# Weight sums of the last projection made in the first layer and stored, and attention units recorded to end one chunk ahead of their host

## The chip, the cores and the metric

The kernel runs on one core of one Trainium2 chip. The metric is the device time of one execution in microseconds (us). Engines are named as the profile names them: PE (TensorE matmuls), PEld (its weight loads), DVE (VectorE), ACT (ScalarE), POOL (GpSimd), SP (SyncE, which issues every DMA of this kernel).

## What is computed

A decoder trunk of two layers on x, 1024 positions of 1024 features, float32. The reference, cut:

```python
for i in range(DEPTH):                          # DEPTH = 2
    if i < N_A_LAYERS:                          # layer 0: retention, 4 heads, qk 256, v 512
        u = rms_norm(h, ret_norm_pre[i])
        q, k, v, g = jnp.split(u @ ret_w_in[i], ...)
        o = retention_chunkwise(rope(q), rope(k) * 256 ** -0.5, v)      # per head, normed
        y = (merge_heads(o) * silu(g)) @ ret_w_out[i]                   # first output projection
        h = h + rms_norm(y, ret_norm_post[i])
        k_sh, v_sh = jnp.split(rms_norm(h, kv_norm) @ w_kv, [SB_QK_WIDTH], axis=-1)
    else:                                       # layer 1: stick-breaking attention, 8 heads
        q, g = jnp.split(rms_norm(h, sb_norm_pre[j]) @ sb_w_in[j], [SB_QK_WIDTH], axis=-1)
        z = q @ k_sh.T * scale
        A = sigmoid(z) * (product of 1 - sigmoid(z) over the later keys), strictly causal
        y = (merge_heads(A @ v_sh) * silu(g)) @ sb_w_out[j]             # second output projection
        h = h + rms_norm(y, sb_norm_post[j])
```

## The kernel before

Each of the large products is a 2x2 block product done with seven block products instead of eight (numbered 1 to 7), each operand of which is a sum or difference of blocks. Every float32 operand is split into a rounded part ("hi") and the rest ("lo"), and a product is three matmuls (`mm3`: hi by hi, hi by lo, lo by hi). ACT makes the hi part, DVE the lo part.

The class `Out` does an output projection (2048 to 1024). It has 28 units `(n, i)`: block product n in the order 1, 5, 3, 6, 7, 4, 2, and i, one of four quarters of the block's 1024 contracted rows. For a unit, `weights(n, i)` loads one or two blocks of 128 x 1024 into tiles `raw`, adds them on DVE where the product needs a sum, and splits the result into a tile `whl`; `operand(n, i)` does the same for the activations (`raw` to `op`, or to `AT` for n = 2). The sums of the weights are w10+w11 for product 5, w10+w11+w00 for 6, w01 plus that for 3, and w10+w00 for 7: four adds of 128 x 1024 for each i. `Out` is used twice: in the first layer (base 48) and at the end of the second (base 112, operands `oc`). A unit is two chunks (`kk`) of 4 x 3 matmuls of 512 columns.

The class `Group` does the input projections, six groups in each layer: in the first layer v0, g0, k, q, v1, g1 (in this order, with the products 2 and 7 of v0, g0 and v1 ahead of all), in the second K, Q, V0, G0, V1, G1.

Attention in the second layer goes by 16 units: 8 pairs of heads and position halves `(t, pr)`, two heads `hh` each. For a unit, `CPair.rows` makes four row blocks of 128 queries: scores on PE (tile `pz` from `ko`, `ko`), two sigmoids on ACT into tiles `n` (named `sgn`, or `f` for t = 0) and `a` (named `A`, or `f`), two causal selects on POOL, then on DVE a running product over `sgn` (a scan) and the product `A<-A,sgn`. `CPair.mix` then turns blocks of A with PE transposes (`pz<-ident,A`), splits them into `AT` (ACT hi, DVE lo), and multiplies with the values into `po`; at its end `gate` multiplies `po` with the gate into `S` and stores it to `oc`. Units with t = 1 have 1024 keys and are the heavy ones.

Attention has no stage of its own: it is recorded between the chunks of a host by `merge(main, *sides)`. Each side is `(steps, lead, tail)`; after chunk i of the host's len(main), as many of the steps are recorded as their share of the chunks from `lead` to len(main) - `tail`. While unit k is mixed, the rows of unit k + 1 are made (`head(k)`). Units 0 to 3 are hosted by V1's products, units 4 to 7 by G1's, units 8 to 15 by half products of the last projection, four chunks each.

What is recorded is not yet the order on the engines. `Recorder` keeps the list of operations, and `Plan` simulates the engines with costs written by hand and gives every engine its order: PE may take an operation from up to 100 ahead, the other engines take whichever of their ready operations has the earliest deadline. `limits` makes the deadlines backwards from the time of the PE operations. Tiles come from tagged pools of a fixed number of buffers: `raw` shares a pool of 28 with `xh`, `v`, `A`, `AT`, `S`, `ko` and `sgn`. The instruction stream of an engine is fixed by this, and so is SP's order of DMAs.

Of the kernel before, what the change touches and what calls it, by code (L numbers as in the profile page):

```python
# [10 lines left out]
F32 = mybir.dt.float32  # L11
F32R = mybir.dt.float32r
AF = mybir.ActivationFunctionType
ALU = mybir.AluOpType
# [26 lines left out]
DMA_QUEUE = 2000.0  # L41
DMA_TIME = 4000.0
PE_AHEAD = 100


class Tile:
# [95 lines left out]
class Recorder:  # L142
    def __init__(self, nc):
        self.nc, self.ops, self.turning, self.placed = nc, [], False, set()
        for e, name in enumerate(ENGINES):
            setattr(self, name, Engine(self, e, name))

# [7 lines left out]
    def add(self, engine, method, args, kw):  # L155
        o = Op()
        o.i, o.engine, o.method, o.args, o.kw = len(self.ops), engine, method, args, kw
        views = [x for x in list(args) + list(kw.values()) if isinstance(x, View)]
        out, also = args[0], kw.get("accum_out")
        o.deps, o.tiles = set(), []  # L160
        for x in views:
            if x.tile not in o.tiles:
                o.tiles.append(x.tile)
        for x in views:
            t, m, w = x.tile, x.mask(), x is out or x is also
            for j, jm, jw in t.log:
                if jm & m and (w or jw):
                    o.deps.add(j)
        for x in views:
            t, m, w = x.tile, x.mask(), x is out or x is also  # L170
            if w:
                t.log = [(j, jm & ~m, jw) for j, jm, jw in t.log if jm & ~m]
            t.log.append((o.i, m, w))
        o.deps.discard(o.i)
        self.cost(o, out, [x for x in views if x is not out and x is not also])
        for t in o.tiles:
            t.users += 1
        self.ops.append(o)
# [102 lines left out]
class Plan:  # L281
# [23 lines left out]
                        self.reuse[j].append(first)  # L305
    def limits(self, when, end):
        late = [0.0] * len(self.ops)
        for o in reversed(self.ops):
            x = when[o.i] if o.engine == PEE else end
            took = DMA_TIME if o.engine == SPE else o.took  # L310
            for j in self.succ[o.i]:
                x = min(x, late[j] - took - 40)
            for j in self.reuse[o.i]:
                x = min(x, late[j] - took - 40)
            late[o.i] = x
        return late
# [140 lines left out]
def trunk(ctx, tc, xT, wts, gains, trig, ident_in, cols, grow_in, out):  # L457
# [471 lines left out]
    class Out:  # L929

        def __init__(self, base, o_d, turned, y, put):
            self.base, self.o_d, self.turned, self.y, self.put = base, o_d, turned, y, put
            self.units = [(n, i) for n in (1, 5, 3, 6, 7, 4, 2) for i in range(4)]
            self.get = ahead(28, lambda at: (self.weights(*self.units[at]), self.operand(*self.units[at])))
            self.banks, self.kept, self.s, self.x = {}, {}, {}, {}

        def pieces(self, x):
            return x[:, 0, :], x[:, 1, :]

        def weights(self, n, i):  # L940

            def load(j, half):
                raw = S("raw", [1024])
                dma(raw[:], wts[self.base + 8 * j + 4 * half + i])
                return raw

            def plus(a, b):
                V.tensor_tensor(a[:], a[:], b[:], ALU.add)
                return a

            w = S("whl", [2, 1024], F32R)
            if n in (1, 2, 4):
                a = load(*{1: (0, 0), 2: (0, 1), 4: (1, 1)}[n])
            elif n == 7:
                a = plus(load(1, 0), load(0, 0))
            elif n == 6:
                a = self.s[i]
            elif n == 5:
                a = self.s[i] = plus(load(1, 0), load(1, 1))
            else:  # L960
                a = plus(self.s[i], load(0, 0))
                a = plus(load(0, 1), a)
            split(self.pieces(w), a[:])
            return w
# [576 lines left out]
    def run():  # L1541
# [24 lines left out]
        def unit(k):  # L1566

            def sides():
                x = [(U[k].mix() + U[k].give + U[k].gate(), 0, 0)]
                if k < 7:  # L1570
                    x.append((U[k + 1].scores(), 0, 0))
                return x
            return sides
        main = groups[0].chunks(2)
        X.load(1, 0, (1,))
        X.unnormed(1, 0)
# [15 lines left out]
        for at, group in enumerate(groups):  # L1592
# [7 lines left out]
            else:  # L1600
                if at == 2:
                    X.tables()
                go(group.chunks(*order[at]))
        hold, acc = [[None] * 4 for _ in range(2)], [[], []]

        def held(t, j, b):
# [22 lines left out]

        def head(k):  # L1630
            h, hh = seq[k]
            x = [(P[h].mix(hh), 0, 0)]
            if k + 1 < len(seq):
                h, hh = seq[k + 1]
                x.append((P[h].rows(hh), 0, 0))
            return x
        for at, group in enumerate(groups[:4]):
            go(group.chunks(*order[at]), (lambda: [(late[2:], 0, 16)]) if at == 0 else None)
        for at, first in ((4, 0), (5, 4)):
            n = order[at]  # L1640
# [1 line left out]
            for k in range(4):  # L1642
                go(groups[at].chunks(n[k + 1]), lambda k=k: head(first + k))
            go(groups[at].chunks(n[5]))
        turns, done = zip(*[finish(t) for t in range(2)])
        Y = Out(112, oc_d, True, lambda t, j, b: S("f2", [512])[:], lambda t, j, b, y: done[t](j, b, y))
        for k, n in enumerate((1, 5, 3, 6)):
            for half in range(2):
                go(Y.chunks(n)[4 * half:4 * half + 4], lambda k=k, half=half: head(8 + 2 * k + half))
# [69 lines left out]
```

## Time and profile before

| what | value |
|---|---|
| time, median of three runs (lowest, highest) | 1589.07 us (1587.85, 1589.58) |
| the profiled execution: its time, its span | 1590.58 us, 1588.8 us |
| PE busy in the span | 1572.9 us, 7416 matmuls |
| DVE busy | 1306.5 us, 1909 instructions |
| ACT, POOL busy | 831.1 us, 230.2 us |
| DMA, mean | 253 GB/s, 401.62 MB |

The span reaches from the first to the last instruction; the execution's time has 1.8 us more. A matmul in the records lasts longer than the next one has to wait, so two matmuls overlap in the records, and "busy" is the union. What a stall of PE takes is read from the starts of neighbouring matmuls.

### The profile page before, as it was taken

The page shows a single profiled execution, that of the slowest core. Times are in us where ns is not written, and L with a number is a line of the kernel's source. Part 1 is how long each engine was busy: PE and PEld are TensorE (multiplying, and loading weights), DVE is VectorE, ACT ScalarE, POOL GpSimd, SP SyncE. Part 2 cuts the span into 40 slices and gives each one's busy share as a digit, 9 for nine tenths or more (in the row PEclk, how much of TensorE's full clock was granted, in tenths as well). Part 3 has the DMA queues.
Part 4 walks back from the last instruction along what each step waited for, and adds up shares of the span by engine and source line. Part 5 has one row for each costly group of instructions (what it writes and reads, how often), then busy time and mean ns, then how long its engine had stood idle before and what let it go on. Part 6 is the DMA issues. An engine that isn't in the chain of part 4 may idle for free. (4 is left out here: it accounts for less than half of the span.)

```text
span 1588.8 us, 22243 instructions
## 1 busy us (share of the span) xinstructions
PE 1572.9 (99%) x7416; PEld 1303.5 (82%) x7416; DVE 1306.5 (82%) x1909; ACT 831.1 (52%) x1470; POOL 230.2 (14%) x298
## 2 busy tenths in 40 slices
PE   9999999999999999999999999999999999999998
PEld 7888888888887888888888888888888888878886
DVE  6997779797677988999989856757778889899897
ACT  7643432323566665546665554545555654455464
POOL 0000015140022432310000000001211211222000
PEclk9999999999999999999999999999999999999999
DMA  8775737388457887875686968768789778787674
GB/s 286 250 250 184 232 113 232 113 279 290 164 175 241 301 334 273 311 299 171 202 301 231 335 218 318 251 223 280 267 283 338 266 278 285 299 291 270 253 268 156
DMA packets 173490, 401.62 MB, mean 253 GB/s; under 512 B 19520, under 2 KB 20160, under 8 KB 173376
## 3 DMA queue, kind: packets, MB, share of 16 engines
q1 hardware_dynamic: 173376, 400.21, 71.5%
q8 instruction: 58, 0.95, 0.2%
q14 instruction: 56, 0.46, 0.1%
HBM read 295.28 MB, written 104.86 MB: 252 GB/s over the span
## 5 line engine op out<-in xcount | busy, mean ns | idle before, releaser
L228 ACT ACTIVATE whl<-wraw 128x512 fp32r<-128x512 f32 (+1 forms) x264 | 157.3, 626 | 233.8 <-PE po L228 69.9
L228 DVE TENSOR_TENSOR whl<-wraw,whl 128x512 fp32r<-128x512 f32 x264 | 183.7, 720 | 92.1 <-ACT whl L228 91.2
L228 PE MATMUL pma<-whl,xh 128*128 128x512 f32 x480 | 126.3, 394 | 0.7 <-DVE whl L228 0.5
L228 PE MATMUL pmb<-whl,xh 128*128 128x512 f32 x480 | 123.6, 390 | 0.0
L228 PE MATMUL pma<-xh,whl 128*128 128x512 f32 x408 | 104.8, 391 | 0.8 <-DVE f L228 0.8
L228 PEld LDWEIGHTS pmb<-whl,xh 128*128 128x128 f32 x480 | 89.8, 188 | 18.6
L228 PE MATMUL pmb<-xh,whl 128*128 128x512 f32 x408 | 104.7, 390 | 0.0
L228 PEld LDWEIGHTS pma<-whl,xh 128*128 128x128 f32 x480 | 88.2, 188 | 18.9 <-DVE whl L228 0.9
L228 PE MATMUL pz<-ko,ko 128*128 128x384 f32 (+3 forms) x480 | 96.2, 327 | 0.0
L228 POOL TENSOR_SCALAR_AFFINE_SELECT f<-f 128x128 f32<-128x128 f32 x64 | 35.3, 566 | 405.1 <-DMA g<-sg 285.2
L228 ACT ACTIVATE AT<-pz 128x512 fp32r<-128x512 f32 (+1 forms) x96 | 45.0, 490 | 89.6 <-PE pz L228 88.9
L228 PEld LDWEIGHTS pma<-xh,whl 128*128 128x128 f32 x408 | 76.1, 188 | 16.7 <-DVE f L228 1.2
L228 POOL TENSOR_TENSOR f<-f,f 128x512 f32<-128x512 f32 x32 | 53.2, 1672 | 252.4 <-DVE f L228 225.1
L228 PE MATMUL pma<-op,whl 128*128 128x512 f32 x336 | 89.5, 396 | 0.0
L228 PEld LDWEIGHTS pmb<-xh,whl 128*128 128x128 f32 x408 | 76.2, 188 | 15.8 <-DVE f L228 0.2
L228 DVE SCALAR_TENSOR_TENSOR wraw<-wraw,gn,wraw 128x512 f32<-128x512 f32 x96 | 71.0, 746 | 19.7 <-ACT wraw L228 9.5
L228 PE MATMUL pmb<-op,whl 128*128 128x512 f32 x336 | 86.5, 391 | 0.0
L228 PEld LDWEIGHTS pz<-ko,ko 128*128 128x128 f32 x480 | 76.3, 190 | 11.7 <-DVE AT L228 1.7
L228 DVE TENSOR_TENSOR wraw<-wraw,wraw 128x512 f32<-128x512 f32 x96 | 69.9, 747 | 13.2 <-DMA wraw<-in_wts_dram 12.8
L228 PE MATMUL pz<-xh,whl 128*128 128x512 f32 x312 | 79.4, 389 | 0.0
L228 PE MATMUL po<-xh,whl 128*128 128x512 f32 x312 | 79.2, 389 | 0.0
L228 PE MATMUL pma<-whl,op 128*128 128x512 f32 x288 | 78.4, 399 | 0.0
(220 smaller groups left out, 3654.5 us busy)
## 6 DMA issues: line engine op xcount, KB each, us to landing
wraw<-in_wts_dram SPq DMA_DIRECT2D x431, 256.0 KB, 5.1
raw<-in_wts_dram SPq DMA_DIRECT2D x72, 512.0 KB, 7.0
v<-v SPq DMA_DIRECT2D x64, 512.0 KB, 5.3
ko<-kq SPq DMA_DIRECT2D x40, 512.0 KB, 5.7
raw<-o SPq DMA_DIRECT2D x36, 512.0 KB, 7.0
raw<-oc SPq DMA_DIRECT2D x36, 512.0 KB, 6.2
kq<-v SPq DMA_DIRECT2D x32, 512.0 KB, 6.5
s<-f SPq DMA_DIRECT2D x40, 256.0 KB, 3.1
```

Source lines behind the costliest of these rows:

```text
L228: f(*[_real(a) for a in o.args], **{k: _real(v) for k, v in o.kw.items()})
```

## The change

It has two parts. First, `Out.add(i)` makes the four weight sums of the second layer's projection for one i: it loads the four blocks, adds them in place with four DVE instructions, and stores each sum to a DRAM tile `ws`. The four calls are recorded in the first layer beside the rest of g0 (i = 0), k (i = 1, 2) and q (i = 3); their operations are marked `filler`, and `limits` gives a filler a deadline of its own, 15 us (`FILL`, in ns) behind the next PE operation in the recorded order. `weights` then loads the stored sum where there is one. So 16 adds leave the last projection, its weight loads go from 36 to 28 (the 16 sums, and 12 plain blocks), and 16 adds, 16 loads and 16 stores, of 512 KB each, are new in the first layer. Second, `head` gives both of its sides a tail of 1: a unit's mixing and the next unit's rows are recorded over the host's chunks but the last.

```diff
+FILL = 15000.0
...
     def limits(self, when, end):
         late = [0.0] * len(self.ops)
+        turn = end
         for o in reversed(self.ops):
-            x = when[o.i] if o.engine == PEE else end
+            if o.engine == PEE:
+                turn = when[o.i]
+            x = when[o.i] if o.engine == PEE else min(end, turn + FILL) if o.filler else end
...
+        def load(self, j, half, i):
+            raw = S("raw", [1024])
+            dma(raw[:], wts[self.base + 8 * j + 4 * half + i])
+            return raw
+
+        def add(self, i):
+            rec.filler = True
+            a, b, c, d = [self.load(j, half, i) for j, half in ((1, 0), (1, 1), (0, 0), (0, 1))]
+            for n, x, y in ((5, b, a), (7, a, c), (6, c, b), (3, d, c)):
+                V.tensor_tensor(x[:], x[:], y[:], ALU.add)
+                self.sums[n, i] = DRAM(f"ws{self.base}{n}{i}", F32)
+                dma(self.sums[n, i][:], x[:])
+            rec.filler = False
...
         def weights(self, n, i):
...
-            if n in (1, 2, 4):
+            if (n, i) in self.sums:
+                a = S("raw", [1024])
+                dma(a[:], self.sums[n, i][:])
+            elif n in (1, 2, 4):
...
+        Z = Out(112, oc_d, True, lambda t, j, b: S("f2", [512])[:], lambda t, j, b, y: done[t](j, b, y))
...
-                go(group.chunks(*order[at]))
+                go(group.chunks(*order[at]), (lambda at=at: [([Z.adds()[i] for i in {1: (0,), 2: (1, 2), 3: (3,)}[at]], 2, 2)]) if at in {1: (0,), 2: (1, 2), 3: (3,)} else None)
...
         def head(k):
             h, hh = seq[k]
-            x = [(P[h].mix(hh), 0, 0)]
+            x = [(P[h].mix(hh), 0, 1)]
             if k + 1 < len(seq):
                 h, hh = seq[k + 1]
-                x.append((P[h].rows(hh), 0, 0))
+                x.append((P[h].rows(hh), 0, 1))
...
-        Y = Out(112, oc_d, True, lambda t, j, b: S("f2", [512])[:], lambda t, j, b, y: done[t](j, b, y))
+        Y = Z
```

Both parts move instructions through the planner. PE's order is the same as before from the start up to the first of the second layer's attention units (about 1105 us in the profile), and another from there on. DVE's, ACT's and SP's orders differ in the first layer from about 112 us to 312 us, are the same up to about 1100 us, and differ from there. POOL's instructions stand in the same order of kinds throughout. In the rows below a name is the program's (`A2544` is the tile `A` number 2544; what follows the underscore is the build's own number); tiles of the two kernels have different numbers.

The first place is PE where a heavy unit begins to be mixed, the first of those hosted by the last projection (about 1403 us before). Before:

```order
L228 MATMUL pma2460_13448<-whl2528_13822,op2532_13794 128x512
L228 MATMUL pma2461_13454<-whl2528_13822,op2532_13794 128x512 x3
L228 MATMUL pmb2462_13466<-whl2528_13822,op2532_13794 128x512 x3
L228 MATMUL pmb2463_13472<-whl2528_13822,op2532_13794 128x512 x3
L228 MATMUL pz2554_13898<-ident_68,A2544_13873 128x128
L228 MATMUL pz2557_13903<-ident_68,A2544_13873 128x128
L228 MATMUL po2569_13939<-AT2555_13933,vo2553_13732 128x512
```

and after, on the same engine, at the same unit:

```order
L231 MATMUL pma2475_13541<-whl2545_13780,op2548_13788 128x512 x2
L231 MATMUL pmb2476_13549<-whl2545_13780,op2548_13788 128x512 x2
L231 MATMUL pz2564_13983<-ident_68,A2551_13931 128x128
L231 MATMUL pz2567_13986<-ident_68,A2551_13931 128x128
L231 MATMUL pmb2476_13549<-whl2545_13780,op2548_13788 128x512
L231 MATMUL pmb2477_13555<-whl2545_13780,op2548_13788 128x512 x3
L231 MATMUL po2572_14020<-AT2565_14010,vo2563_13666 128x512
```

The transposes of the unit's last row block stood right ahead of the first product `po` that needs them; now four of the host's matmuls stand between.

The second place is DVE ahead of the same point (about 1392 to 1405 us before): the scans and products that make the last two row blocks. Before:

```order
L228 TENSOR_TENSOR AT2534_13786<-pz2533_13781,AT2534_13786 128x128
L228 TENSOR_TENSOR raw2530_13683<-raw2530_13683,raw2436_13041 128x1024
L228 TENSOR_TENSOR A2524_13756<-A2524_13756,sgn2525_13751 128x767
L228 TENSOR_TENSOR op2532_13794<-raw2531_13741,op2532_13794 128x1024
L228 TENSOR_TENSOR whl2528_13822<-raw2530_13683,whl2528_13822 128x1024
L228 SCALAR_TENSOR_TENSOR sgn2536_13813<-sgn2536_13813 128x896
L228 TENSOR_TENSOR S2543_13881<-po2520_13726,sg2522_13704 128x512
L228 TENSOR_TENSOR S2543_13881<-po2521_13734,sg2523_13717 128x512
L228 TENSOR_TENSOR A2535_13817<-A2535_13817,sgn2536_13813 128x895
L228 SCALAR_TENSOR_TENSOR sgn2545_13867<-sgn2545_13867 128x1024
L228 TENSOR_TENSOR raw2455_13192<-raw2455_13192,raw2549_13808 128x1024
L228 TENSOR_TENSOR A2544_13873<-A2544_13873,sgn2545_13867 128x1023
```

and after:

```order
L231 SCALAR_TENSOR_TENSOR sgn2527_13800<-sgn2527_13800 128x640
L231 TENSOR_TENSOR A2526_13806<-A2526_13806,sgn2527_13800 128x639
L231 SCALAR_TENSOR_TENSOR sgn2539_13849<-sgn2539_13849 128x768
L231 TENSOR_TENSOR A2538_13855<-A2538_13855,sgn2539_13849 128x767
L231 TENSOR_TENSOR S2549_13904<-po2532_13804,sg2534_13646 128x512
L231 TENSOR_TENSOR S2549_13904<-po2533_13811,sg2535_13659 128x512
L231 TENSOR_TENSOR whl2559_13892<-raw2560_13840,whl2559_13892 128x1024
L231 SCALAR_TENSOR_TENSOR sgn2543_13874<-sgn2543_13874 128x896
L231 SCALAR_TENSOR_TENSOR sgn2552_13926<-sgn2552_13926 128x1024
L231 TENSOR_TENSOR A2542_13881<-A2542_13881,sgn2543_13874 128x895
L231 TENSOR_TENSOR A2551_13931<-A2551_13931,sgn2552_13926 128x1023
L231 TENSOR_TENSOR op2562_13936<-raw2561_13858,op2562_13936 128x1024
```

The two weight adds (`raw<-raw,raw`) that stood in this stretch are gone, and the scans of the last two row blocks stand directly behind each other.

The third place is DVE in the first layer, beside g0 (about 146 to 152 us before). Before:

```order
L228 TENSOR_TENSOR whl271_1747<-wraw253_1548,whl271_1747 128x512
L228 TENSOR_TENSOR whl271_1747<-wraw256_1591,whl271_1747 128x512
L228 TENSOR_TENSOR wraw277_1736<-wraw277_1736,wraw243_1464 128x512
L228 SCALAR_TENSOR_TENSOR f2264_1775<-f2258_1613,col102_864,f2263_1770 128x512
L228 SCALAR_TENSOR_TENSOR f2266_1782<-f2259_1644,col102_864,f2265_1777 128x512
```

and after:

```order
L231 TENSOR_TENSOR raw297_1691<-raw297_1691,raw296_1590 128x1024
L231 TENSOR_TENSOR raw296_1590<-raw296_1590,raw298_1703 128x1024
L231 TENSOR_TENSOR whl271_1772<-wraw253_1566,whl271_1772 128x512
L231 TENSOR_TENSOR whl271_1772<-wraw256_1614,whl271_1772 128x512
L231 TENSOR_TENSOR raw298_1703<-raw298_1703,raw297_1691 128x1024
L231 TENSOR_TENSOR raw361_1750<-raw361_1750,raw360_1732 128x1024
L231 TENSOR_TENSOR wraw277_1776<-wraw277_1776,wraw243_1480 128x512
L231 SCALAR_TENSOR_TENSOR f2264_1819<-f2258_1660,col102_880,f2263_1800 128x512
```

Four of the 16 new adds are set between the splits of g0's weights. Counted along DVE's order, 13 of the 16 stand ahead of what ran at about 228 us before, the other three where 247 to 275 us were.

More of the change, by code (lines that the diff above doesn't have):

```diff
@@ L144, in __init__ @@
         self.nc, self.ops, self.turning, self.placed = nc, [], False, set()
+        self.filler = False
         for e, name in enumerate(ENGINES):
@@ L157, in add @@
         o.i, o.engine, o.method, o.args, o.kw = len(self.ops), engine, method, args, kw
+        o.filler = self.filler
         views = [x for x in list(args) + list(kw.values()) if isinstance(x, View)]
@@ L935, in __init__, with adds @@
             self.banks, self.kept, self.s, self.x = {}, {}, {}, {}
+            self.sums = {}
         def pieces(self, x):
             return x[:, 0, :], x[:, 1, :]
+        def load(self, j, half, i):
[10 more added lines that the diff above has]
+            rec.filler = False
+        def adds(self):
+            return [lambda i=i: self.add(i) for i in range(4)]
         def weights(self, n, i):
             def load(j, half):
-                raw = S("raw", [1024])
-                dma(raw[:], wts[self.base + 8 * j + 4 * half + i])
-                return raw
+                return self.load(j, half, i)
             def plus(a, b):
@@ L1573, in unit @@
             return sides
+        turns, done = zip(*[finish(t) for t in range(2)])
+        Z = Out(112, oc_d, True, lambda t, j, b: S("f2", [512])[:], lambda t, j, b, y: done[t](j, b, y))
         main = groups[0].chunks(2)
@@ L1644, in run @@
             go(groups[at].chunks(n[5]))
-        turns, done = zip(*[finish(t) for t in range(2)])
-        Y = Out(112, oc_d, True, lambda t, j, b: S("f2", [512])[:], lambda t, j, b, y: done[t](j, b, y))
+        Y = Z
         for k, n in enumerate((1, 5, 3, 6)):
```

## Prediction

> **What bounds the kernel now.** I read the page first, then busy time by stretches, then PE's waits, then PE's and DVE's instructions around each wait.
>
> ```profile
> span 1588.8 us, 22243 instructions
> PE 1572.9 (99%) x7416; PEld 1303.5 (82%) x7416; DVE 1306.5 (82%) x1909; ACT 831.1 (52%) x1470; POOL 230.2 (14%) x298
> ```
>
> PE is the bound: 15.9 us of the span are without a matmul, and neither part of the change adds or removes a matmul. So only PE's stalls can move the time. By stretches (length, then busy time and count of each engine, granted clock, DMA share, GB/s):
>
> ```profile
> 10.00:1095.00 1085.00, 1082.08 (x4945) 894.88 (x4944) 884.26 (x1358) 558.52 (x938) 150.64 (x166) 1.00 0.70 245
> 1190.00:1250.00 60.00, 58.44 (x291) 47.75 (x291) 53.86 (x70) 37.75 (x75) 10.25 (x14) 1.00 0.87 313
> 1408.00:1412.00 4.00, 4.00 (x17) 3.35 (x16) 3.45 (x3) 1.51 (x6) 1.74 (x2) 0.57 0.79 261
> 1582.00:1589.00 7.00, 0.12 (x1) 0.00 (x0) 2.96 (x5) 1.02 (x3) 0.00 (x0) 0.76 0.20 75
> ```
>
> 6.9 us are the end behind the last matmul, which the change leaves alone; 2.9 us lie in the 1085 us before the second layer's attention. What remains is short, and sits in the attention's stretch. PE's waits from 1095 us to the end (total, times, longest), and below them the one kind that the first layer's hosted units (430 to 700 us) show:
>
> ```profile
> PE po L228 <- ACT AT L228: 1.7, 3, 0.6
> PE pz L228 <- DVE A L228: 0.9, 1, 0.9
> PE pma L228 <- DVE f L228: 0.8, 1, 0.8
> PE po L228 <- ACT sgn L228: 2.1, 3, 0.9
> ```
>
> Matmuls overlap in the records, so a wait costs more than its idle time; the loss is read from starts. The pace of 128x512 matmuls that wait for nothing, from the chain at the end, is 11.00/48 = 0.229 us:
>
> ```profile
> 1560.25 11.00 PE pma L228 x48
> ```
>
> PE's instructions in order of time, at the five places that lose most (start, length, what, idle before and its releaser):
>
> ```profile
> 1190.98 2.89 PE L228 MATMUL pma<-xh,whl 128*128 128x512 f32 x12
> 1194.66 1.66 PE L228 MATMUL pma<-xh,whl 128*128 128x512 f32 x6 [0.79 <-DVE f L228]
> ...
> 1223.27 0.86 PE L228 MATMUL pma<-xh,whl 128*128 128x512 f32 x3
> 1224.33 0.30 PE L228 MATMUL pz<-ident,A 128*128 128x128 f32 x1 [0.20 <-DVE AT L228]
> ...
> 1237.35 0.38 PE L228 MATMUL pz<-ident,A 128*128 128x128 f32 x2
> 1238.31 0.73 PE L228 MATMUL po<-AT,vo 128*128 128x512 f32 x2 [0.58 <-ACT AT L228]
> ...
> 1403.27 1.55 PE L228 MATMUL pmb<-whl,op 128*128 128x512 f32 x6
> 1405.67 0.44 PE L228 MATMUL pz<-ident,A 128*128 128x128 f32 x2 [0.85 <-DVE A L228]
> 1406.69 0.74 PE L228 MATMUL po<-AT,vo 128*128 128x512 f32 x2 [0.58 <-ACT AT L228]
> ...
> 1411.08 1.24 PE L228 MATMUL pz<-ident,A 128*128 128x128 f32 x8
> 1412.08 1.86 PE L228 MATMUL po<-AT,vo 128*128 128x512 f32 x7
> ...
> 1437.25 0.38 PE L228 MATMUL pz<-ident,A 128*128 128x128 f32 x2
> 1438.21 0.73 PE L228 MATMUL po<-AT,vo 128*128 128x512 f32 x2 [0.58 <-ACT AT L228]
> ```
>
> Losses, start to start: (a) where G1's matmuls follow V1's, 1194.66 - 1190.98 - 12 x 0.229 = 0.93 us; (b) 1224.33 - 1223.27 - 3 x 0.229 = 0.37 us; (c) transposes straight ahead of the `po` that needs them, three times: 0.96, 1.02 and 0.96 us, of which two transposes may take 2 x 1.00/8 = 0.25 (the row of eight), so 0.71 + 0.77 + 0.71 = 2.19 us; (d) the late row block, 1405.67 - 1403.27 - 6 x 0.229 = 1.03 us; (e) behind it the granted clock is 0.57 over 4 us (the third stretch above), which loses 4 x 0.43 = 1.72 us. Sum: 6.24 us.
>
> What made (d) late stands in DVE's order of time:
>
> ```profile
> 1398.82 1.26 DVE L228 TENSOR_TENSOR S<-po,sg 128x512 f32<-128x512 f32 x2
> 1400.00 1.07 DVE L228 TENSOR_TENSOR A<-A,sgn 128x895 f32<-128x895 f32 x1
> 1400.99 2.37 DVE L228 TENSOR_TENSOR_SCAN sgn<-sgn 128x1024 f32<-128x1024 f32 x1
> 1403.29 1.19 DVE L228 TENSOR_TENSOR raw<-raw,raw 128x1024 f32<-128x1024 f32 x1
> 1404.41 1.21 DVE L228 TENSOR_TENSOR A<-A,sgn 128x1023 f32<-128x1023 f32 x1
> ```
>
> DVE runs without a pause there, and a weight add of 1.12 us (start to start) stands between the last scan and the product that PE's transposes wait for.
>
> **The adds leave the last projection.** In the stretch that hosts attention and the last projection, DVE is busy
>
> ```profile
> 1376.00:1560.00 184.00, 181.99 (x934) 151.38 (x932) 169.23 (x188) 104.90 (x192) 24.52 (x34) 0.99 0.76 277
> L228 DVE TENSOR_TENSOR raw<-raw,raw 128x1024 f32<-128x1024 f32 x18 | 21.9, 1220 | 0.0
> ```
>
> 169.2 of 184 us (92%). Of these 18 adds, those of weights go (16 in the whole projection, 16 x 1.22 = 19.5 us). DVE falls to some 82 to 85%. Eight weight loads of 512 KB go as well. Taking the adds away ends (d): the product could start 1.12 us earlier, more than the 1.03 us lost, and DVE's rows of the new order show five adds fewer between the storing of the unit before (`S`) and this product. With (d) go the two holes in 3 us that stand ahead of the slow clock, so (e) goes too. Together 2.75 us.
>
> [...]
>
> **The tail of one chunk.** A unit's rows end a chunk earlier, and its host's last chunk stands alone behind them. PE's rows of the new order show it twice. Where a heavy unit begins, four host matmuls stand between the last transposes and the first `po` (in the seven heavy hand-offs: four each, five once). They cover 4 x 0.229 = 0.92 us, against holes of 0.71 to 0.77: all of (c) goes, 2.19 us. And where G1 follows V1, PE before ran four groups of three matmuls into one bank while it waited for DVE to empty another; now the banks follow each other in turn, and the last scores stand some 40 host matmuls earlier, so DVE's scans no longer collide with emptying the banks: (a) goes, 0.93 us. For (b), a transpose late by 0.37 us, bounds are 0 and 0.37; I take 0.37, since DVE has less to do there too. What is late next: the last two row blocks, whose scans now stand back to back (below).
>
> **The adds in the first layer.** 16 adds, 16 loads and 16 stores are new where PE waits for nothing. The room:
>
> ```profile
> 125.00:235.00 110.00, 110.00 (x487) 91.13 (x486) 79.69 (x122) 42.61 (x74) 6.68 (x4) 1.00 0.53 176
> 235.00:310.00 75.00, 75.00 (x332) 62.12 (x331) 64.28 (x88) 23.45 (x40) 26.34 (x16) 1.00 0.55 183
> 349.88 1.67 POOL L228 TENSOR_TENSOR f<-f,f 128x512 f32<-128x512 f32 x1 [7.93 <-DVE f L228]
> 350.31 1.78 DVE L228 TENSOR_TENSOR wraw<-wraw,wraw 128x512 f32<-128x512 f32 x1
> ```
>
> DVE is idle 30.3 us in the first stretch, which gets 13 adds (15.9 us), and 10.7 us in the second, which gets three (3.7 us). The 32 transfers are 16.8 MB; at 176/0.53 = 332 GB/s they take 51 us, and DMA is free for 0.47 x 110 + 0.45 x 75 = 85 us. SP issues 32 more DMAs, and a store that waits for its add holds the weight loads behind it, for the length of an add or two. The last two rows show the danger, an add that took 1.78 us beside one of 1.67 on POOL. POOL is busy 6.7 us in the first stretch; if all of it falls on new adds they take 15.9 + 6.7 = 22.6 of the 30.3 us. In the second, one POOL add on each of the three makes 3.7 + 5.0 = 8.7 of 10.7. I cost this part at 0; what hides it is the weights made ahead, and without that cover an add late by its whole length costs 1.2 us each. Bounds: 0 to 3 us lost, a gain excluded, since PE has no hole there to fill.
>
> **The sum.** 6.24 us of losses go. A new order has holes of its own: none seen at the hand-offs, so 0 is one end; the other is the first layer's hosted units, 2.1 us of waits in 270 us, which over the 494 us from 1095 on is 3.8 us. I take 1.0, nearer to 0, because the hand-offs are covered by rows of the order. Net 6.24 - 1.0 = 5.2 us. On the profiled execution (1590.58 us, its span 1588.8 and 1.8 around it) that gives 1585.4; the median of the runs shown is 1.5 us below it, and I predict 1589.07 - 5.2 = 1583.9 us.
>
> **Rivals.** Against the median, 0.2% (3.2 us) is about what a measurement of this kernel can tell from no change.
>
> *Moved, not removed.* The new order has as many holes as the hosted units of the first layer, 3.8 us, or (e) comes back at another hole: gain 6.24 - 3.8 = 2.4 us, 1586.7 us. For it: PE's order is new over 494 us, and a single hole pair like 1403 to 1412 costs 1.03 + 0.77 + 1.72 = 3.5 us. Against: every heavy hand-off has its cover.
>
> *The slow clock stays.* If (e) hangs on something other than the holes ahead of it, 5.2 - 1.7 = 3.5 us are left, 1585.6 us. The row speaks against it, and no other row for it; a chance of 0.08, inside the forecast's.
>
> *Nothing of the adds.* DVE is at 92% either way one may say, and (d) is the latency of scan and product; then only (a) and (c) go, 3.1 us: 1586.0 us. Against it stands the add of 1.12 us in the row itself.
>
> *Slower.* The last two row blocks' scans stand back to back: 2.37 us of the last scan and the product of the block before (1.07) now lie between a scan and its own product. If at the heavy hand-offs the last product comes later than PE's transposes, each costs a hole and a clock drop like (d) with (e), 2.75 us, and from the third on the change loses: 6.24 - 4 x 2.75 = -4.8, so four of seven give 1593.8 us. For it: the order's pairs. Against: the last product there has no add ahead of it, and its transposes stand later on PE than before.
>
> *All goes and nothing comes:* 6.24 us and up to 2 us more of small waits between: 1581 to 1583 us.
>
> **Chances.** Forecast (gain 3.2 to 6.2 us) 0.48; all goes 0.18; moved or nothing of the adds 0.26, of which a little lies above 3.2; slower 0.08. Faster by over 0.2%: 0.67; within: 0.25; slower: 0.08. The likeliest case's own range is 1582.9 to 1585.9; the range that leaves out the slower case and the outer half of "all goes" is 1580.8 to 1589.4.
>
> **What the profile after would show.** PE's waits from 1095 us: no `po` on `AT` at 0.58, no `pz` on `A`, sum below 1.5 us instead of 3.6; granted clock 1.00 up to the last matmul; DVE at 82 to 85% from 1376 to 1560 us; in the first layer raw adds beside PE at 100%. The prediction is wrong if PE waits for `whl` between 125 and 350 us, if the clock drops at another place, or if `pz` waits for `A` at the hand-offs.

## The result and the profile after

The changed kernel takes 1583.89 us (median of six runs, 1582.14 to 1585.25), beside 1589.32 us for the kernel before in runs taken with it (1587.85 to 1591.66). The ratio is 0.9966, with a 95% interval of 0.9955 to 0.9976: 5.4 us less. The forecast was 1583.9 us. The profiled execution took 1583.15 us, with a span of 1581.3 us. One further execution of the kernel before, run beside the experiments, took 3201.51 us and is left out of every figure below.

The top of the page of the kernel after:

```profile
span 1581.3 us, 22235 instructions
PE 1570.2 (99%) x7416; PEld 1302.4 (82%) x7416; DVE 1308.4 (83%) x1909; ACT 830.1 (52%) x1470; POOL 225.9 (14%) x298
```

PE's and DVE's busy times hardly differ from before (1572.9 and 1306.5 us); 11.1 us of the span are now without a matmul, where 15.9 us were. What moved stands in the stretches. Kernel after, busy time by stretches, in the columns of the prediction's:

```profile
1190.00:1250.00 60.00, 60.00 (x302) 49.40 (x302) 50.67 (x69) 36.65 (x72) 7.87 (x12) 1.00 0.86 306
1400.00:1412.00 12.00, 12.00 (x65) 9.82 (x64) 8.63 (x12) 7.01 (x13) 0.54 (x2) 1.00 0.89 330
1376.00:1560.00 184.00, 184.00 (x950) 153.05 (x949) 158.97 (x188) 107.35 (x202) 17.61 (x33) 1.00 0.69 252
125.00:235.00 110.00, 110.00 (x487) 91.10 (x487) 92.93 (x133) 41.66 (x72) 6.54 (x4) 1.00 0.88 307
235.00:310.00 75.00, 75.00 (x333) 62.13 (x331) 69.32 (x91) 23.49 (x40) 28.54 (x16) 1.00 0.63 208
```

In the 60 us around G1's beginning PE has no idle time left (before: 1.6 us), nor in the 184 us of the last projection (before: 2.0 us); the granted clock is 1.00 there, and in the 12 us around the hand-off where four had 0.57. In the first layer DVE is busy 13.2 us longer in the first of the two stretches with new adds (92.93 - 79.69) and 5.0 us in the second (69.32 - 64.28), and PE is busy for the whole of both. The new adds there, first those from 125 to 235 us, then from 235 to 310 us:

```profile
L231 DVE TENSOR_TENSOR raw<-raw,raw 128x1024 f32<-128x1024 f32 x13 | 15.7, 1217 | 0.1
...
L231 DVE TENSOR_TENSOR raw<-raw,raw 128x1024 f32<-128x1024 f32 x3 | 4.7, 1579 | 0.0
```

PE's waits in the kernel after: first those from 10 to 1095 us, then the only one from 1095 us on:

```profile
PE po L231 <- ACT sgn L231: 2.0, 3, 0.9
PE pma L231 <- DVE whl L231: 0.5, 1, 0.5
PE pz L231 <- ACT on L231: 0.2, 1, 0.2
...
PE pmb L231 <- DVE f L231: 0.4, 1, 0.4
```

From 1095 us on 3.6 us of waits became 0.4 us. The same places as in the prediction, in PE's order of time: the hand-off at 1400 us, and the place where G1's matmuls follow V1's.

```profile
1400.64 0.38 PE L231 MATMUL pz<-ident,A 128*128 128x128 f32 x2
1400.78 1.17 PE L231 MATMUL pmb<-whl,op 128*128 128x512 f32 x4
1401.79 0.62 PE L231 MATMUL po<-AT,vo 128*128 128x512 f32 x2
1402.25 0.40 PE L231 MATMUL pma<-whl,op 128*128 128x512 f32 x1
...
1188.68 1.52 PE L231 MATMUL pmb<-whl,xh 128*128 128x512 f32 x6
1190.04 1.52 PE L231 MATMUL pma<-xh,whl 128*128 128x512 f32 x6
1191.40 0.84 PE L231 MATMUL pmb<-xh,whl 128*128 128x512 f32 x3
```

Four matmuls of the host, 1.01 us start to start, stand where PE idled before the first `po`. At G1 groups of six alternate between the banks `pmb` and `pma` at 1.36 us each (six times 0.227 us), without a gap. DVE ahead of the hand-off:

```profile
1395.57 2.29 DVE L231 TENSOR_TENSOR_SCAN sgn<-sgn 128x1024 f32<-128x1024 f32 x1 [0.39 <-POOL sgn L231]
1397.78 2.25 DVE L231 TENSOR_TENSOR A<-A,sgn 128x895 f32<-128x895 f32 x2
```

The last two products end at 1400.03 us, 0.6 us ahead of the transposes that read the last one (1400.64), although their scans stand back to back.

### The profile page after: what moved, and what is told of

Read it like the earlier page. It is cut to its first block, busy times and chain, and to the rows that moved or that the text cites. A ratio compares the mean times of both kernels' runs of the same rounds, so it can differ in the third digit from the quotient of the medians.

```text
span 1581.3 us, 22235 instructions
## 1 busy us (share of the span) xinstructions
PE 1570.2 (99%) x7416; PEld 1302.4 (82%) x7416; DVE 1308.4 (83%) x1909; ACT 830.1 (52%) x1470; POOL 225.9 (14%) x298
## 4 chain that ended last, share of the span: by engine, by line
PE 96%; DVE 2%; DMA 1%; issue 1%; ACT 0%; POOL 0%; DVEq 0%; SPq 0%; POOLq 0%
PE pma L231 28%; PE pmb L231 28%; PE po L231 22%; PE pz L231 18%; DMA wraw<-in_wts_dram 1%; DVE f L231 0%; DVE wraw L231 0%; POOL small L231 0%; DMA f<-av 0%; DVE small L231 0%; DVE whl L231 0%; ACT sgn L231 0%; ACT whl L231 0%; ACT v L231 0%; DVE sg L231 0%
## 5 line engine op out<-in xcount | busy, mean ns | idle before, releaser
L231 POOL TENSOR_TENSOR f<-f,f 128x512 f32<-128x512 f32 x32 | 56.7, 1785 | 248.9 <-DVE f L231 238.1
L231 POOL TENSOR_SCALAR_AFFINE_SELECT f<-f 128x128 f32<-128x128 f32 x64 | 31.3, 508 | 408.3 <-ACT f L231 391.6
L231 ACT ACTIVATE AT<-pz 128x512 fp32r<-128x512 f32 (+2 forms) x96 | 45.3, 489 | 83.0 <-PE pz L231 81.6
L231 DVE TENSOR_TENSOR_SCAN sgn<-sgn 128x640 f32<-128x640 f32 (+3 forms) x32 | 61.7, 1928 | 19.1 <-POOL sgn L231 18.9
```

The source lines that it names most:

```text
L231: f(*[_real(a) for a in o.args], **{k: _real(v) for k, v in o.kw.items()})
```

## Experiments

Each ratio is to the kernel before, run beside it on the same chip (medians there 1589.0, 1588.83 and 1588.67 us). The ratios are the measurement's own and differ from the quotients of these medians by up to 0.0006. Before the runs one thing for several of them: every execution has 7416 matmuls, so the start of matmul number n cuts any of the kernels at about the same amount of work. Counted from the traces, the time between four such marks is (us):

| kernel | 5000 to 5700 (V1, G1) | 5700 to 6500 | 6500 to 6700 (first heavy hand-offs in the last projection) | 6700 to the end |
|---|---|---|---|---|
| before, again | 141.36 | 154.24 | 42.05 | 147.53 |
| before, first profile | 141.14 | 154.19 | 43.64 | 147.57 |
| after | 138.82 | 154.16 | 38.63 | 148.17 |
| adds only | 141.91 | 154.23 | 38.74 | 147.94 |
| tail only | 138.84 | 154.17 | 42.53 | 148.37 |
| tail in groups alone | 138.13 | 154.58 | 43.66 | 147.99 |
| adds, tail in groups | 138.50 | 154.48 | 38.73 | 147.89 |
| before's order, no adds | 140.73 | 154.25 | 41.17 | 147.57 |

Orders differ, so a mark stands among slightly different matmuls; some tenths of a microsecond between neighbouring columns mean nothing.

**The kernel before, once more** (no edit).

> The kernel before once more, unchanged, for a second profile of it. Theory (the slow clock behind the late row block comes in some executions only, and the profile of before was one with it and with a late first weight): no stretch at half clock within the matmuls, the same three kinds of waits from 1095 us on, and a span of 1586 to 1588 us. Rival (the slow clock comes every time): a stretch at half of 3.4 us at about 1408 us again, span near 1588.5. Ratio 1.000 within 0.0010 by both, which shows what the comparison can tell.

1589.16 us, ratio 1.0002 (0.9993 to 1.001). In this execution, PE's instructions at the same holes, and the clock of the 4 us behind the pair at 1407 us:

```profile
1191.96 2.90 PE L228 MATMUL pma<-xh,whl 128*128 128x512 f32 x12
1195.63 1.66 PE L228 MATMUL pma<-xh,whl 128*128 128x512 f32 x6 [0.77 <-DVE f L228]
1197.13 2.90 PE L228 MATMUL pmb<-xh,whl 128*128 128x512 f32 x12
...
1239.32 0.73 PE L228 MATMUL po<-AT,vo 128*128 128x512 f32 x2 [0.58 <-ACT AT L228]
1240.05 1.14 PE L228 MATMUL pz<-ko,ko 128*128 128x512 f32 x5
...
1406.72 0.44 PE L228 MATMUL pz<-ident,A 128*128 128x128 f32 x2 [0.85 <-DVE A L228]
1407.74 0.74 PE L228 MATMUL po<-AT,vo 128*128 128x512 f32 x2 [0.58 <-ACT AT L228]
1408.46 1.25 PE L228 MATMUL pz<-ko,ko 128*128 128x512 f32 x6
...
1437.67 0.73 PE L228 MATMUL po<-AT,vo 128*128 128x512 f32 x2 [0.58 <-ACT AT L228]
1438.24 0.63 PE L228 MATMUL pma<-whl,op 128*128 128x512 f32 x2
```

```profile
1408.00:1412.00 4.00, 4.00 (x23) 3.13 (x23) 4.00 (x5) 3.10 (x8) 1.22 (x2) 1.00 0.87 308
```

The holes of 0.85 and 0.58 us are the same to the hundredth, and the clock stays at 1.00. In the first profile it was 0.57 there, and matmuls 6500 to 6700 took 1.59 us more. The span is only 0.6 us shorter (1588.2 us), because this execution came to matmul 5000 0.8 us later. So the slow clock belongs to some executions of this program only. How many, the mean granted clock of each whole execution tells, which a stretch like that lowers by 1.7/1589, a thousandth: of 67 executions of the kernel before, here and beside the other runs, 18 have a mean of 0.998 and the others 0.999 or more. In the four sets that they were run in, the medians are 1589.8 to 1590.7 us for the first and 1588.2 to 1589.1 us for the second, 1.3 to 2.3 us apart. Both profiles fit (0.998 with the drop, 0.999 without). In all the profiles together the mean is below 0.9985 where the clock fell within the matmuls and above it where it did not (0.9984 and 0.9986 at the closest). Of the 49 executions of the kernel after, adds only, tail only, before's order without the adds, after's order without the first layer's part, and adds with the tail in groups, none is below 0.999; of the tail in groups alone, whose profile has the drop too, 4 of 11 are. Of the five executions with a tail in the first layer too (below), which has no wait of PE from 1095 us on, one is: it took 1586.13 us at 0.998, where the other four took 1581.35 to 1583.48. It was not the profiled one, so where its clock fell is not known.

These rows show a second thing: the two `po` behind a hole hold the next matmul up for 0.73, 0.72 and 0.57 us, where the kernel after takes 0.46 (1401.79 to 1402.25 above). Read matmul by matmul, the first `po` behind each hole takes 0.34 us to the next start instead of 0.23. At the first two places a second wait follows: the trace names DVE's `AT` as what released `pz<-ko,ko`, which starts at 1408.46 us, just behind the first of the two instructions in this row of DVE (it ended at 1408.41).

```profile
1407.73 1.28 DVE L228 TENSOR_TENSOR AT<-pz,AT 128x512 fp32r<-128x512 f32 x2
```

The records show no idle time there, since the `po` ahead still counts as busy: in the first profile it starts at 1407.03 us and lasts 0.40 us in the records, past the start of the `pz` at 1407.41.

**The adds alone.** The kernel after, both tails of `head` back to 0:

```diff
-            x = [(P[h].mix(hh), 0, 1)]
+            x = [(P[h].mix(hh), 0, 0)]
...
-                x.append((P[h].rows(hh), 0, 1))
+                x.append((P[h].rows(hh), 0, 0))
```

> The weight sums are made in the first layer as in the changed kernel, but the attention units keep a tail of 0. Theory (adds and tail end different holes): PE's order of this kernel has four host matmuls between the last transposes and the first po at the hand-offs hosted by the last projection, none at the first heavy one hosted by G1, and G1's first matmuls still pile four groups into one bank. So the late row block at about 1403 us (1.03 us), the slow clock behind it (1.72 us) and two of the three holes ahead of po (0.77 + 0.71 us) go, 4.2 us of the 6.2; the hole where G1 follows V1 (0.93 us), the late transpose (0.37 us) and one hole ahead of po (0.71 us) stay. Ratio about 0.9973. Rival (the prediction's own split: all holes ahead of po belong to the tail): 2.75 us, ratio 0.9983. Rival (the tail does all): no gain, 1.000.

1586.0 us, ratio 0.9984 (0.9975 to 0.9993). PE's waits from 1095 us:

```profile
PE pz L231 <- DVE f L231: 1.2, 1, 1.2
PE pma L231 <- DVE f L231: 0.8, 1, 0.8
PE po L231 <- ACT AT L231: 0.6, 1, 0.6
PE pz L231 <- DVE AT L231: 0.2, 1, 0.2
```

All four lie ahead of 1250 us; the last projection has none. Of the three waits of `po` on `AT` one is left, the one under G1. So the two in the last projection, and the late row block, go with the adds. The wait of `pma` on `f`, where G1 follows V1, stays. The waits are those of the theory, the ratio is not its 0.9973: it counted 1.72 us for the slow clock, which most executions don't have, and V1 and G1 took 0.55 us more here (141.91 against 141.36 us). That the ratio is close to the rival's 0.9983 is chance, since the waits aren't the rival's.

**The tail alone.** The kernel before, both tails of `head` at 1:

```diff
-            x = [(P[h].mix(hh), 0, 0)]
+            x = [(P[h].mix(hh), 0, 1)]
...
-                x.append((P[h].rows(hh), 0, 0))
+                x.append((P[h].rows(hh), 0, 1))
```

> The tail of 1, with the weight sums still made in the last projection. Theory: the hole where G1 follows V1, the late transpose and the first hole ahead of po go, 0.93 + 0.37 + 0.71 = 2.0 us, ratio about 0.9987; at the first two hand-offs in the last projection PE's order has no host matmuls ahead of po, so two waits of po on AT at about 0.58 us stay, and the late row block with the slow clock may stay. Rival (prediction's split): all three holes ahead of po and (a) go, 3.1 us, ratio 0.9980. Rival (the adds do all): 1.000.

1587.01 us, ratio 0.9992 (0.9983 to 1.0001), not told apart from no change. The longest of PE's waits from 1095 us:

```profile
PE po L228 <- ACT AT L228: 1.2, 2, 0.6
PE pz L228 <- DVE AT L228: 0.7, 1, 0.7
PE pz L228 <- ACT A L228: 0.5, 1, 0.5
```

The mirror image: V1 and G1 have the whole gain (138.84 us, as in the kernel after), and the last projection keeps both of its waits of `po` on `AT`. The late row block is on time here too (no `pz` waits for DVE's `A`), but two other waits of `pz` are new, the one on ACT's `A` ahead of that hand-off (1395 to 1400 us) and the one on `AT` at 1420 to 1440 us, so the stretch gains nothing (42.53 against 42.05 us). The hole of 0.73 us before that `pz` and one of 0.58 us stand 0.7 us apart, a pair like the one at the late row block, and none of the 11 executions is below 0.999. Counted in PE's order, the host matmuls between a heavy unit's last transposes and its first `po` are, for the eight heavy units in turn: before 0, 0, 4, 4, 0, 0, 4, 4; adds only 0, 0, 4, 4, 4, 4, 4, 4; tail only 2, 4, 4, 5, 0, 0, 3, 4; after 2, 4, 4, 5, 4, 4, 4, 4. The cover at the fifth and sixth comes with the adds, whatever the tail.

**The tail where it helps.** The kernel before with the tail for units 0 to 7 only (those hosted by V1 and G1), and the kernel after with the same restriction:

```diff
             h, hh = seq[k]
+            tail = 1 if k < 8 else 0
-            x = [(P[h].mix(hh), 0, 0)]
+            x = [(P[h].mix(hh), 0, tail)]
...
-                x.append((P[h].rows(hh), 0, 0))
+                x.append((P[h].rows(hh), 0, tail))
```

> The kernel before with the tail of 1 for units 0 to 7 alone (those hosted by V1 and G1); the adds and the units in the last projection stay as before. Theory (the tail's worth lies in the stage of V1 and G1, and without the adds moved it costs something in the last projection): the hole where G1 follows V1, the late transpose and the first hole ahead of po go, and nothing else changes: 2.0 to 2.5 us, ratio about 0.9985, faster than the tail on all units (0.9992). Rival (the tail's gain is spread over all units): no faster than the tail on all units, 0.9992 or more.

1586.98 us, ratio 0.9987 (0.9978 to 0.9996).

> The changed kernel with the tail of 1 for units 0 to 7 alone; units 8 to 15, in the last projection, have a tail of 0. Theory (with the adds gone the tail is worth nothing in the last projection): the time of the changed kernel, ratio 0.9966 within 0.0007, PE's waits from 1095 us below 1 us. Rival (the tail makes the cover in the last projection): waits of po on AT of 0.58 us come back there and 1 to 1.5 us are lost, ratio about 0.9975.

1583.35 us, ratio 0.9964 (0.9952 to 0.9977), and no wait of PE from 1095 us on. With the adds moved, the tail in the last projection is worth nothing that can be measured. Without them its table row says it costs (42.53 + 148.37 against 42.05 + 147.53, 1.3 us), but the two times overlap within their intervals, so this stays open. The profiled execution of the first of the two met the slow clock, behind its own pair of holes:

```profile
1403.58 0.44 PE L228 MATMUL pz<-ident,A 128*128 128x128 f32 x2 [0.70 <-DVE A L228]
1404.60 0.73 PE L228 MATMUL po<-AT,vo 128*128 128x512 f32 x2 [0.58 <-ACT AT L228]
```

```profile
1405.50:1409.50 4.00, 4.00 (x14) 3.24 (x15) 3.77 (x4) 1.90 (x5) 1.47 (x2) 0.57 0.77 268
```

**Before's order without the weight adds.** All engines keep the order of the kernel before; the 16 adds are left out when the instructions are written:

```diff
     def emit(self, order):
         for o in order:
+            if o.left_out:
+                continue
...
             def plus(a, b):
+                rec.left_out = self.base == 112
                 V.tensor_tensor(a[:], a[:], b[:], ALU.add)
+                rec.left_out = False
```

> The kernel before in its own order on every engine, with the 16 weight adds of the last projection left out of DVE's stream and nothing put in their place (the loads stay; the products 5, 7, 6 and 3 get a block in place of a sum). Theory: only what DVE's time does goes: the late row block (1.03 us) and the slow clock behind it (1.72 us), 2.75 us, ratio 0.9983; PE's waits of po on AT stay at three of about 0.58 us and the hole where G1 follows V1 stays. Rival (the row block's delay is scan and product, not the add): the wait of pz on A stays above 0.5 us and the ratio is above 0.9993. Rival (the clock falls for another reason): the wait goes and the clock record still has a stretch at half within the matmuls, ratio 0.9993.

1588.1 us, ratio 0.9997 (0.9988 to 1.0007): no change that can be measured. The interval leaves out the theory's 0.9983, which again counted the slow clock; a gain of up to 1.9 us fits it, and the table's row sums to 1.5 us less than that of before. The longest of PE's waits from 1095 us, and the stretch of the last projection:

```profile
PE po L232 <- ACT AT L232: 1.8, 3, 0.6
PE pma L232 <- DVE f L232: 0.8, 1, 0.8
```

```profile
1376.00:1560.00 184.00, 182.78 (x942) 152.11 (x941) 158.25 (x179) 108.52 (x201) 26.76 (x34) 1.00 0.75 277
```

The wait of `pz` on `A` is gone, as the add of 1.12 us ahead of the product was to explain. The three waits of `po` are untouched, although DVE is as free as in the kernel after (158 of 184 us). With PE's order fixed, 0.9 us came back from matmul 6500 to 6700 (41.17 against 42.05), not the 3.4 us of the real change.

**More DVE work in either order.** The kernel before with each of the 16 adds issued twice; and the kernel after with 16 adds of 128 x 1024 put back in the last projection, one ahead of the split of each stored sum:

```diff
-            f(*[_real(a) for a in o.args], **{k: _real(v) for k, v in o.kw.items()})
+            for _ in range(2 if o.twice else 1):
+                f(*[_real(a) for a in o.args], **{k: _real(v) for k, v in o.kw.items()})
...
+            if o.ahead is not None:
+                a = _real(o.ahead)
+                self.nc.vector.tensor_tensor(a, a, a, ALU.add)
```

(The first two added lines are the first kernel's, the last three the second's.)

> The kernel before in its own order, each of the 16 weight adds of the last projection issued twice in a row (the sums come out wrong). Theory (the delay at the hand-offs is DVE's time, and a hole of this size drops the clock): the wait of pz on A at about 1403 us grows from 0.85 to about 2.0 us, other hand-offs with an add in their stretch get waits of their own of up to 1 us, and the clock record shows a stretch at half behind them: 2 to 5 us slower than before, ratio 1.001 to 1.003. Rival (from the run without the adds, whose time moved by 0.5 us only: DVE's time there is not what counts): 1.000 within 0.0005.

1605.42 us, ratio 1.0106 (1.0091 to 1.0122), far beyond both expectations.

> The changed kernel in its own order, with 16 adds of 128 x 1024 put back on DVE in the last projection, each right ahead of the split of a stored sum (a tile added to itself, so the output is another). The first layer's adds stay. Theory A (the gain is PE's order, with host matmuls as cover): most of the gain stays, ratio 0.9966 to 0.9975, with waits of pz on A of some tenths where an add falls into a hand-off. Theory B (the gain is DVE's time itself): the gain of the adds, 2.5 to 4 us, is lost again, ratio 0.998 or more, with waits of pz on A and po on AT from 1376 us on.

1601.67 us, ratio 1.0084 (1.0071 to 1.0098). Theory A, that the gain stays, missed; the ratio falls in theory B's, but the loss against the kernel after is more than four times what B named. The longest of PE's waits from 1095 us, of the first and then of the second:

```profile
PE pz L231 <- DVE A L231: 5.1, 4, 3.0
PE pz L231 <- DVE AT L231: 3.5, 5, 1.3
```

```profile
PE pz L234 <- ACT A L234: 3.8, 5, 1.4
PE pz L234 <- DVE AT L234: 3.3, 6, 0.9
PE po L234 <- DVE AT L234: 2.8, 2, 2.1
```

The clock fell in both profiles too. The stretch at half clock, of the first and then of the second (there the 8 us from 1512 us have a mean granted clock of 0.79):

```profile
1412.60:1422.84 10.24, 8.39 (x25) 6.31 (x26) 8.21 (x9) 4.42 (x9) 1.33 (x2) 0.50 0.68 233
```

```profile
1515.70:1519.00 3.30, 3.30 (x10) 2.53 (x9) 2.17 (x4) 0.00 (x0) 0.00 (x0) 0.50 0.51 173
```

19.5 us of DVE work more cost 16.6 us in before's order and, by the medians, 17.8 us in after's; of this the slow clock has up to 10.24 x 0.5 = 5.1 and 8 x 0.21 = 1.7 us in the profiled executions. In before's order 19.5 us less were worth nothing that could be measured. So in these two fixed orders added work cost much of its length, directly and through the clock, and work that went gave little back. Other orders, and other places for the adds, were not tried. After's cover of four matmuls did not shield it from these adds, so this pair of runs does not tell by itself whether the gain is PE's order or DVE's time; that rests on the adds alone (38.74 us from matmul 6500 to 6700) against before's order without them (41.17 us).

**After's order without the first layer's part.** The 4 x 4 loads, 16 adds and 16 stores are left out of the instructions, and `weights` loads a plain block where it loaded a stored sum:

```diff
         for o in order:
+            if o.filler:
+                continue
...
                 dma(a[:], self.sums[n, i][:])
+                rec.ops[-1].instead = wts[self.base + i].bitcast(F32)
```

> The changed kernel in its own order, with the first layer's 16 adds, 16 loads and 16 stores left out, and the last projection loading a plain block in place of each stored sum. Theory (the first layer hides them at no cost): the same time as the changed kernel, ratio 0.9966 within 0.0007; PE's waits before 1095 us stay at 2.0 + 0.5 + 0.2 us. Rival (the fillers cost 1 us or more in the first layer): ratio 0.9960 or less, and shorter waits or an earlier pace there.

1583.04 us, ratio 0.9968 (0.9955 to 0.998), the same as the kernel after. PE's waits before 1095 us are those of the kernel after to the tenth (2.0, 0.5 and 0.2 us). The stretch with 13 of the adds:

```profile
125.00:235.00 110.00, 110.00 (x487) 91.09 (x486) 79.56 (x121) 42.01 (x73) 6.61 (x4) 1.00 0.53 174
```

DVE is 13.4 us lower than with the fillers, and DMA's share 0.53 instead of 0.88, and PE is busy for the whole stretch either way: the first layer takes the fillers in at no cost that the runs can show.

**A tail in the first layer too.** The kernel after, with a tail of 1 for the hosted units of retention:

```diff
-                x = [(U[k].mix() + U[k].give + U[k].gate(), 0, 0)]
+                x = [(U[k].mix() + U[k].give + U[k].gate(), 0, 1)]
...
-                    x.append((U[k + 1].scores(), 0, 0))
+                    x.append((U[k + 1].scores(), 0, 1))
```

> The changed kernel, with a tail of 1 for the retention units of the first layer too. Theory (a tail covers the hand-offs there as well): the three waits of po on ACT's sgn (2.0 us) go, ratio 0.9966 - 0.0013 = 0.9953. Rival (these waits come from the norm's chain behind po, which a tail doesn't shorten): the waits stay within 0.5 us and the ratio is 0.9966 within 0.0007.

1582.97 us, ratio 0.9965 (0.9952 to 0.9977): no gain over the kernel after. PE's waits from 10 to 1095 us:

```profile
PE pma L231 <- ACT whl L231: 1.2, 1, 1.2
PE po L231 <- ACT sgn L231: 0.7, 2, 0.5
PE po L231 <- ACT f L231: 0.7, 1, 0.7
PE pma L231 <- DVE whl L231: 0.6, 1, 0.6
PE po L231 <- ACT ko L231: 0.3, 1, 0.3
```

The waits of `po` on `sgn` fell from 2.0 to 0.7 us, and others took their place (3.5 us in all, where the kernel after has 2.7). This is what the prediction's rival "moved, not removed" describes, at a place where it did happen.

So the theory is right in the main on those waits, and the rival on the time. None of these kernels beats the kernel after by more than the intervals.

## Why the prediction was right, point by point

**The time.** 5.4 us were measured and 5.2 forecast. That they are so close is luck: two terms were wrong and one was missing. The slow clock, 1.72 us, is worth next to nothing on the median; the 1.0 us taken off for new holes did not come; and 0.77 us were not counted. 1.0 + 0.77 nearly cancels 1.72. Against the second execution of the kernel before, the gain from matmul 5000 to the end is 485.18 - 479.78 = 5.40 us. It is made up so: (a) to (d), 0.93 + 0.37 + 2.19 + 1.03 = 4.52 us by the prediction's sizes, and 0.77 us that it didn't count, the slower starts behind the holes and, at two of them, the second wait. That is (0.73 - 0.46) + (0.72 - 0.46) + (0.57 - 0.46) = 0.64 us at the three `po`, and 1.50 - 6 x 0.229 = 0.13 us at G1's first six matmuls. Together 5.29 us, 0.1 us short. (The `pz` behind each second wait starts slow again, 0.34 and 0.33 us to the next start in the first profile, 0.1 us each above the pace, which would make it 0.1 us over.) (The two profiled executions differ by 7.4 us; of this 0.7 us are ahead of matmul 5000, where executions of the kernel before already differ by 0.8 us, and the slow clock is 1.6.)

**(a), where G1 follows V1: right.** `pma` no longer waits for `f`; the tail alone brings the stage to the time of the kernel after (138.84 against 141.36 us), the adds alone don't (141.91).

**(b), the late transpose: taken as gone, and not measured apart.** It lies in the same stage, which gained 2.5 us where (a), (b) and the first cover of (c) with the starts behind them make 0.93 + 0.37 + 0.71 + 0.27 + 0.13 = 2.41 us.

**(c), the three covers: the mechanism right, the part of the change wrong for two of them.** Four host matmuls do stand ahead of `po` and no `po` waits. But I read the cover off the new order as the tail's doing. The tail alone leaves the two in the last projection at 0 matmuls and 0.6 us each; the adds alone bring them to 4. The step that failed is "the tail of one chunk ... all of (c) goes". Of its 2.19 us the tail has 0.71 and the moved adds 1.48, by way of the planner, which sets PE's order differently when the adds are elsewhere. The kernel before had four host matmuls ahead of `po` at four of the eight hand-offs already, so the rows of the new order alone could not tell which part of the change set the others.

**(d), the late row block: right.** It goes when only the adds are left out of before's order, with nothing else moved. (The tail alone, which moves the rows, ends it too, and other waits come.)

**(e), the slow clock: the term that was mis-sized.** 1.72 us is what it cost in one profiled execution. In another of the same kernel the same two holes left the clock at 1.00. It happens in about a quarter of the executions (18 of 67), so it is worth some 0.26 x 1.72 = 0.45 us on the mean and next to nothing on the median. It went from all but one of the 54 executions of kernels without the pair of holes at the late row block; the one, with a tail in the first layer too, speaks against the pair as its only cause, and the pair in the tail alone (0.73 and 0.58 us), where none of the 11 executions is below 0.999, shows that two such holes are not enough. In the first profile the clock was at 0.50 from 1408.08 to 1411.49 us, 1.4 us behind the end of the second hole (1406.69 us), and at 1.00 everywhere else within the matmuls; there and in the tail for V1 and G1 alone it came down behind gaps below 0.9 us (0.85 and 0.58, 0.70 and 0.58 us). I took one execution's drop for what the holes do. The two holes are 1.43 us of idle time in each of the two executions of the kernel before. Why the clock fell in one and not in the other stays open.

**New holes: 1.0 us forecast, none found.** From 1095 us 0.4 us of waits are left, a `pmb` on `f` at 1106 us, and the kernel before has its like there (0.37 us of idle time at 1107 us in its second execution). The bound I scaled from, the first layer's hosted units, was no measure for units that are covered. The balance above closes within 0.1 us, so new holes took no more than that, unless other places gave as much back.

**The first layer at 0: right.** The 13 adds took 15.7 us, 15.9 forecast; the three take 4.7 us, 1.58 us each, between the 3.7 forecast and its bound of 8.7 with a POOL add beside each. Without the fillers the time is the same within the interval.

**The views named ahead.** No `po` on `AT`, no `pz` on `A`, waits below 1.5 us, the clock at 1.00 and PE at 100% in the first layer came as said. DVE from 1376 to 1560 us came to 159 of 184 us, 86%, just above the 82 to 85 forecast: PE gets through 950 matmuls in that stretch now, 934 before, so more of DVE's work falls in it.

**The rivals.** "Nothing of the adds" falls: with the tail in V1 and G1, the adds are 1586.98 against 1583.35 us. "Slower", by the paired scans, falls at the rows of DVE above, where the last product is ready 0.6 us ahead of its transposes, and no `pz` waits for `A` at any hand-off. "The slow clock stays" asked the wrong question, since it isn't there in every execution before. "Moved, not removed" is out for this change.

## What to carry to other kernels

In a kernel whose engines follow a planned order, price a moved instruction by where PE's order changes with it, not by the busy time of the engine it leaves: 19.5 us less on DVE gave nothing measurable in this kernel's old order and most of 3 us in the new one, while 19.5 us more cost 16.6 and 17.8 us, a part of it through the slow clock. A cost that stands in one profiled execution, a clock drop above all (18 of 67 executions had it here), needs a second execution of the same kernel before it goes into a sum. A hole on PE is priced through the matmuls behind it, not to the first: here that one took 0.34 us to the next start instead of 0.23, and at two of the three `po` the overlap in the records hid a second wait.

## What the runs showed of the hardware

- The clock fell to 0.50 for 3.41 us behind PE gaps of 0.85 and 0.58 us in one execution of the kernel before, and not in another with the same gaps; behind 0.70 and 0.58 us it fell again (0.57 over 4 us) in the kernel with the tail in V1 and G1 alone, and behind a single gap of 2.08 us in the kernel after with adds put back (0.50 over 3.30 us). By the mean clock 18 of 67 executions of the kernel before show it. In the profiles neither the single gaps of 0.58 us (1239 and 1437 us in the kernel before) nor one of 1.2 us (a `pz` on `f` ahead of 1250 us in the adds alone) brought a drop, nor did a pair of 0.58 and 0.73 us (1433 us in the tail alone).
- The first matmul of 128x512 behind a gap held the next one up for 0.34 us, where the pace is 0.23 us: at ten places in the first profile of the kernel before, behind gaps of 0.15 to 1.07 us, it took 0.335 to 0.342 us, and at five in the kernel after, behind 0.36 to 0.90 us, 0.335 to 0.339 us.
- Work on DVE and DMA in a stretch where PE is fully busy cost PE nothing that the runs can tell, with DVE at 84% (92.93 of 110 us) and DMA at 0.88, and with DVE at 92% (69.32 of 75 us) and DMA at 0.63: PE was busy for 110.00 and 75.00 us, and the kernel took 1583.89 us with the work and 1583.04 without.
